# A DeepNorm encoder layer on one core: 21 of 24 projection chunks in the first stage, seven feature tiles modulated by VectorE

## The chip, the core and the metric

The kernel runs on one core of one Trainium2 chip. The metric is the device time of one execution in microseconds (us). Three timed runs of the kernel before gave 1085.3, 1085.6 and 1085.9 us, a median of 1085.61 us.

A core has a matrix engine, TensorE (PE in the profile, with its weight loads in a row of their own, PEld), a vector engine (DVE), a scalar engine (ACT), GpSimd (POOL) and a sync engine (SP). Each engine works through its own instruction list in the list's order and waits on semaphores for the others. Here almost all weights come through SP's DMA queue, in pieces of 1 MB ("chunks").

## The reference

One encoder layer for 256 tokens of width 2048: windowed attention (32 query heads, 8 key heads, width 64) and a squared-ReLU MLP, both modulated by a condition vector c.

```python
mod = silu(c) @ mod_w + mod_b                        # 2048 -> 6*2048
sh_m, sc_m, g_m, sh_f, sc_f, g_f = split(mod, 6)
h = x * (1 + sc_m) + sh_m
q, k, v = split(h @ w_qkv + b_qkv)                   # 2048 -> 3072
q, k = rope(q), rope(k)
s = where(|kpos - qpos| <= 128, q k^T / 8, -inf)
p = exp(s - m) / (sum(exp(s - m)) + exp(sink - m))
x = LN(2**.25 * x + (1 + g_m) * (p v @ w_o + b_o))
h = x * (1 + sc_f) + sh_f
x = LN(2**.25 * x + (1 + g_f) * (relu(h @ w1 + b1)**2 @ w2 + b2))
```

## The kernel before

**Arithmetic.** A float32 product is made of three fast ones (`mm3`, lines L685 to L687): weights and activations are split into a high part and a rest, and high x high, high x rest and rest x high are summed. So each weight chunk of 128x2048 needs, in two halves, a cast on ACT for the high part (`wh`, L382, in the first stage L393) and a subtraction on DVE for the rest (`wl`, L351), and then 24 matmuls of 128x512.

**First stage.** The 2048 features are 16 tiles of 128 (k = 0 to 15). For each tile, scale and shift must be computed from two chunks of `mod_w` before the tile can be used (`modulated`, L713 to L718). The two chunks are worked off in one of two ways, chosen by `MIXP`: on PE, as 16 small matmuls a chunk (L458, tile `gv`), followed by a copy and a small matmul (L556), or on DVE, as one pass over the whole chunk (L498), two passes a tile. Ten tiles go by PE and six by DVE. Meanwhile the projection to q, k, v runs. Its weight is 24 chunks, 12 of them for the first half of the columns ("units", each of four pieces of one k and 512 columns) and 12 for the other half ("quarters" (g, p): four feature tiles 4g to 4g+3, 512 columns p). `SEQ` lists the chunks that the first stage takes and the tiles whose `mod_w` chunks are loaded behind each: all 12 units and five quarters, 17 chunks. From it `first_order` makes one fixed order for PE, ACT and DVE. Eight buffers of 1 MB feed it; afterwards five are left (`RAWS`).

**Attention.** The other seven projection chunks are in `LATE`. Two of them run ahead of a loop over n = 0 to 20. Step n holds the scores of head pair group n (`scores`: PE L922, DVE L929, ACT L939), the transposes of step n-1's probabilities (`probs_T`: PE L964, ACT L966), the normalising of step n (`normalise`: DVE L947 and L951, ACT L954) and, in every second step, the product with v (`values`: PE L980, ACT L983, DVE L984). Between the pieces a step has one weight chunk of 24 matmuls: in steps 0 to 4 one of the five remaining `LATE` chunks, from step `OUT_AT` = 5 on one of the 16 chunks of the output projection (`project`). Step 5 needs the first two `values`.

**Filling.** What is left of the modulation (the attention gate: 8 row chunks for PE and 8 column chunks for DVE; then the MLP's) is planned into the stream between the weight chunks, `SLOT_FILL` giving how many for each step from n = -2 on: one each for the first seven steps, then two. A row chunk is L458 on tile `pm`, a column chunk L498 on `colm` or `modf`. In the stream row and column chunks alternate. All chunks, of whatever kind, pass through one queue on SP in the planned order, and each waits until its buffer is free.

Outside the fixed first stage, the order on each engine is made by the framework's scheduler when the kernel is built.

Of the kernel before, what the change touches and what calls it, by code (L numbers as in the profile page):

```python
# [20 lines left out]
S = 256  # L21
# [10 lines left out]
PRE = 2  # L32
OUT_AT = 5
X_AT = 11
SLOT_FILL = (1, 1, 1, 1, 1, 1, 1, 2, 2, 2, 2, 2, 2, 2, 2, 2, 2, 2, 2, 2, 1, 0, 0)
MIXG = (1,) * 16
MIXP = tuple(int(k not in (4, 6, 8, 10, 12, 14)) for k in range(16))
FFG = (4, 4, 4, 4)
FFP = (2, 2, 4, 0)
GMP = 1  # L40
# [10 lines left out]
def mod_chunks():  # L51

    out = []
    for which, sizes, prods in (("m", MIXG, MIXP), ("f", FFG, FFP)):
        k0 = 0
        for nk, p in zip(sizes, prods):
            out += [("w" + which, p, k0, i) for i in range(2 * p)]
            out += [("c" + which, n, k, 0) for k in range(k0 + p, k0 + nk) for n in range(2)]
            k0 += nk
    for which, p in (("m", GMP), ("f", 0)):  # L60
        out += [("rg" + which, h, i, 0) for h in range(p) for i in range(8)]
        out += [("cg" + which, 0, k, 0) for k in range(8 * p, NK)]
    return {c: i for i, c in enumerate(out)}


MODS = mod_chunks()
SEQ = [(0, [1, 2]), (1, [3]), (2, []), ((0, 3), [4]), ((0, 4), [5]), (3, [6]), (4, [7]), (5, []), ((1, 3), [8]), ((1, 4), [9]), (6, [10]), (7, [11]), (8, [12]), ((2, 3), [13]), (9, [14]), (10, [15]), (11, [])]
XK = {0: 2, 2: 2, 4: 4, 8: 4, 12: 4}


def first_loads():

    out = [("m", 0, 0), ("m", 0, 1)]
    for n, ks in SEQ:
        out.append(("w", n))
# [4 lines left out]
def first_order():  # L80
# [4 lines left out]
    def op(key, eng, after, rank, kind=None):  # L85
        ops[key] = eng, cost[kind or key[0]], after, rank

    for k in range(NK):
        g0, g1 = ("g", k, 0), ("g", k, 1)
        if MIXP[k]:  # L90
            op(g0, "PE", [("m", k, 0)], 0, "gP")
# [12 lines left out]
    halves, last, freed = [], {"e": [("cp", 3)]}, []  # L104
    for n, _ in SEQ:
        q = type(n) is tuple
# [20 lines left out]
    for i in range(4):  # L127
        op(("sp", i), "PE", [("cp", i - 1)] if i else [("u", SEQ[0][0], 1)], 4)
        op(("cp", i), "ACT", [("sp", i)], 0)
# [39 lines left out]
def hybrid_kernel(ctx: ExitStack, tc: tile.TileContext, a, out: bass.AP):  # L169
# [9 lines left out]
    def bank(name="pa"):  # L179
        return psum.tile([128, 512], F32, name=name, tag="bank")  # L180
# [14 lines left out]
    def g4(dt=F32):  # L195
        return gen.tile([128, 1024], dt, tag="g4", name="g4")
# [99 lines left out]
    def bias_all(src, b):  # L296

        for h in range(2):
            nc.gpsimd.dma_start(b[h], src[:, h * 1024:h * 1024 + 1024].partition_broadcast(128))
        return lambda c: b[c // 2][:, (c % 2) * 512:(c % 2) * 512 + 512]  # L300
# [134 lines left out]
    S = Stream()  # L435
# [169 lines left out]
    def groups(which, sizes, prods, mb, dst):  # L605
        out, k0 = [], 0
        for nk, p in zip(sizes, prods):
            out.append(Group(which, k0, nk, p, mb, dst))
            k0 += nk
        return out  # L610

    modm = cst.tile([128, 2, NK], F32, name="modm")
    modf = cst.tile([128, 2, NK], F32, name="modf")
    m_mix = groups("m", MIXG, MIXP, modmb, modm)
    m_ff = groups("f", FFG, FFP, modfb, modf)
    m_gm = Gate("m", GMP, gateb[:, 0])
    m_gf = Gate("f", 0, gateb[:, 1])

    LATE = [(3, 3), (2, 4), (3, 4), (0, 5), (1, 5), (2, 5), (3, 5)]
    wq = lambda g, p: S.plan(a["wqkv"][12 + (p - 3) * 4 + g])  # L620
    FIRST = first_loads()
    for v in FIRST:
# [11 lines left out]
    def plan_late(n):  # L634
        for _ in range(n):
            while lp[0] < len(late) and late[lp[0]].planned == late[lp[0]].n:
                lp[0] += 1
            if lp[0] < len(late):
                late[lp[0]].plan()

    OUTS = [(c, j) for j in range(4) for c in range(4)]
    for n in range(-PRE, OUT_AT + 16):
        plan_late(SLOT_FILL[n + PRE])
        if n == X_AT:
            S.side[len(S.q)] = lambda: load_rows()
        if n + PRE < len(LATE):
            wq(*LATE[n + PRE])
        elif n >= OUT_AT:
# [35 lines left out]
    def mm3(ps, xh, xl, wh, wl, start, stop):  # L684
        S.pinned(nc.tensor.matmul(ps, xh, wh, start=start, stop=False))  # L685
        nc.tensor.matmul(ps, xh, wl, start=False, stop=False)  # L686
        S.prev = nc.tensor.matmul(ps, xl, wh, start=False, stop=stop).ins  # L687
# [10 lines left out]
    def load_rows():  # L698

        for c in range(4):  # L700
            xs.append(g4())
            nc.sync.dma_start(xs[c].rearrange("p (t n) -> p t n", t=NT), a["x"][:, :, c * 512:c * 512 + 512])
# [80 lines left out]
        else:  # L783
            S.pinned(nc.vector.tensor_add(d, d, ps))

    BEGIN = [(3, 3), (2, 4), (0, 5)]

    def qkv(g, p):

        hh, hl = held[g]  # L790
        wh, wl = S.main()
        c = CORD[p]
        pss = half.pop(c, None) or banks()
        for k2 in (0, 2):
            for t in range(NT):
                for k in (k2, k2 + 1):
                    s = slice(k * 256 + t * 128, k * 256 + t * 128 + 128)
                    mm3(pss[t], hh[:, s], hl[:, s], wh(k), wl(k), k == 0 and (g, p) in BEGIN, False)
            S.done()
            if k2 == 0:  # L800
                yield
        if g < 3:
            half[c] = pss
        else:
            evict(c, pss)

    def run(gen, mid=()):
        next(gen)
        for f in mid:
            f()  # L810
        for _ in gen:
            pass
# [15 lines left out]
    S.loads()  # L828
    nth = {n: i for i, (n, _) in enumerate(SEQ)}
    load_of = {v: i for i, v in enumerate(FIRST)}  # L830
    for op, *v in first_order():
        if op == "g":
            k, i = v
# [19 lines left out]
        elif op == "u":  # L853
            n, i = v
# [14 lines left out]
        S.loads()  # L869
    S.passed(len(FIRST), len(SEQ))  # L870
    S.pin = S.deep = False
# [3 lines left out]
    def rope(c, which):  # L875

        A, B = acc[c], (g4b if late_tiles else g4)()
        Av = A.rearrange("p (t h d) -> p t h d", t=NT, h=8)
        Bv = B.rearrange("p (t h d) -> p t h d", t=NT, h=8)

        def tab(n):
            return trig[:, which, n, :, None, :].to_broadcast([128, NT, 8, 32])

        halves = [slice(0, 32), slice(32, 64)]
        for x in range(2):
            nc.vector.tensor_tensor(Bv[:, :, :, halves[x]], Av[:, :, :, halves[1 - x]], tab(1 + x), op=OP.mult)
        yield A
        for x in range(2):
            nc.vector.tensor_tensor(Av[:, :, :, halves[x]], Av[:, :, :, halves[x]], tab(0), op=OP.mult)
        yield A  # L890
        nc.vector.tensor_add(A, A, B)
        yield A

    def whole(gen):
        for A in gen:
            pass
        return A

    def heads_T(A):

        out = g4()
        for pr in range(2):
            pt = bank("pt")
            for i in range(2):
                for t in range(NT):
                    c = t * 512 + (pr * 2 + i) * 128
                    nc.tensor.transpose(pt[:, i * 256 + t * 128:i * 256 + t * 128 + 128], A[:, c:c + 128], ident)
            nc.scalar.copy(out[:, pr * 512:pr * 512 + 512], pt)
        return out
# [193 lines left out]
    kA = whole(rope(4, 0))  # L1103
    run(qkv(*LATE[0]))
    qA[0] = whole(rope(0, 1))
    kT = []
    run(qkv(*LATE[1]), [lambda: kT.append(heads_T(kA))])
    kT = kT[0]
# [12 lines left out]
    for n in range(OUT_AT + 16):  # L1121
        j, i = n // 4, n % 4
        if n < 16:
            scores(n)
        for f in todo:
            f()
        todo = []
        if n == 3:
            assert all(h is raws for h in S.home[S.at:]), "an early buffer is still in use"
            late_tiles.append(1)  # L1130
        w = iter(())
        if n + PRE < len(LATE):
            w = qkv(*LATE[n + PRE])
        elif n >= OUT_AT:
            if n == OUT_AT:
                bo = bias_all(a["bo"], [g4b(), g4b()])
            w = project(*OUTS[n - OUT_AT])
        mid = mids(n)
        if j < 3:
            if i == 1:  # L1140
                turn = rope(j + 1, 1)
                mid += [lambda: next(turn), lambda: next(turn)]
            if i == 2:
                mid.append(lambda: qA.__setitem__(j + 1, next(turn)))
            if i == 2:
                mid.append(lambda: qT.__setitem__(j + 1, heads_T(qA[j + 1])))
        next(w, None)
        for f in mid:
            f()
        next(w, None)  # L1150
        if 0 < n <= 16 and n % 2 == 0:
            todo.append(values(n - 1))
        if n == 11:
            g1 = m_gm.spread([g4(), g4()])
            st = [sml.tile([128, 4, 6], F32, name=f"st{t}", bufs=2) for t in range(NT)]
        if n == 17:
            ff_columns(0)
# [332 lines left out]
```

## Time and profile before

| What | Number |
|---|---|
| median of three timed runs | 1085.61 us |
| span of the profiled execution, first to last instruction | 1083.7 us |
| PE busy, DVE busy, ACT busy | 98%, 72%, 49% of the span |
| first stage ends on PE (last `mm3` of a unit) | 139.5 us |
| scores of step 0 end on PE | 166.2 us |
| first matmul of the output projection (step 5) | 210.5 us |
| end of the attention and output stage | about 345 us |
| DMA: moved in all, mean rate | 292.75 MB, 270 GB/s |

The page gives one execution on the core; a time of its own beside the span isn't listed, and the span is 1.9 us shorter than the median of the timed runs. Matmul ends are modelled, so a PE that is always busy isn't a PE at its peak; the distance between starts shows the pace.

### The profile page before, as it was taken

To read this page: it belongs to the slowest core of one execution; us is meant where nothing else is said; L and a number is where in the kernel's file an instruction comes from. 1 tells how busy PE (TensorE), PEld (TensorE's weight loads), DVE (VectorE), ACT (ScalarE), POOL (GpSimd) and SP (SyncE) were. 2 spreads that over 40 slices of the span, in tenths; PEclk is the share of its full clock that TensorE was granted. 3 is DMA by queue.
4 is the path that set the end of the run, shared out by engine and by line. 5 is a ranking of instruction groups with operands and counts; after the bars stand their busy time and mean duration, and the time that the engine had idled before them with its cause. 6 is when DMAs were issued, how large, how long until landed. Compare 5 with 4: busy or idle time off the path is not lost.

```text
span 1083.7 us, 16256 instructions
## 1 busy us (share of the span) xinstructions
PE 1064.7 (98%) x6519; PEld 881.5 (81%) x6519; DVE 785.3 (72%) x1134; ACT 527.5 (49%) x814; POOL 19.7 (2%) x41
## 2 busy tenths in 40 slices
PE   8999999999999999999999999999999999999997
PEld 6777776677777899988888888888888888888885
DVE  3587689798799888754688789656665557665795
ACT  2453348777772646633345443344553334554340
POOL 2000000000000000000000010000000000000000
PEclk9999999999999999999999999999999999999999
DMA  9999997898973997555777889756555555557522
GB/s 380 425 425 425 427 407 270 352 348 344 391 277 122 420 352 273 193 194 194 272 272 274 295 293 319 297 203 222 194 194 188 192 193 201 181 181 263 194 78 78
DMA packets 43692, 292.75 MB, mean 270 GB/s; under 512 B 4916, under 2 KB 5076, under 8 KB 9824
## 3 DMA queue, kind: packets, MB, share of 16 engines
q1 hardware_dynamic: 40256, 281.82, 69.3%
q0 software_dynamic: 2496, 8.43, 2.3%
q10 hardware_dynamic: 864, 1.45, 0.4%
q8 instruction: 51, 0.84, 0.3%
q14 instruction: 25, 0.20, 0.0%
HBM read 289.57 MB, written 2.11 MB: 269 GB/s over the span
## 4 chain that ended last, share of the span: by engine, by line
PE 91%; DVE 5%; DMA 1%; ACT 1%; issue 1%; SPq 0%; DVEq 0%; ACTq 0%
PE pa L685 17%; PE pa L687 17%; PE pa L686 16%; PE pa L1264 16%; PE pa L1266 8%; PE pa L1240 3%; PE pa L1238 3%; PE pa L1239 3%; DVE raw L498 2%; PE pm L458 2%; PE gv L458 1%; PE pa L922 1%; PE pt L964 1%; PE pa L980 1%; DMA raw<-in_mod 1%; DVE wl L351 1%
## 5 line engine op out<-in xcount | busy, mean ns | idle before, releaser
L351 DVE TENSOR_TENSOR wl<-raw,wh 128x1024 fp32r<-128x1024 f32 x332 | 403.7, 1222 | 222.4 <-ACT wh L382 205.6
L382 ACT CAST wh<-raw 128x1024 fp32r<-128x1024 f32 x298 | 311.6, 1052 | 346.3 <-PE pa L687 203.1
L685 PE MATMUL pa<-wh,g 128*128 128x512 f32 x816 | 324.1, 398 | 2.7 <-ACT g L782 1.4
L687 PE MATMUL pa<-wh,g 128*128 128x512 f32 x816 | 319.3, 391 | 0.5 <-DVE g L984 0.4
L686 PE MATMUL pa<-wl,g 128*128 128x512 f32 x816 | 319.0, 391 | 0.5 <-DVE wl L351 0.4
L1264 PE MATMUL pa<-g,wh 128*128 128x512 f32 x768 | 192.3, 392 | 0.0
L685 PEld LDWEIGHTS pa<-wh,g 128*128 128x128 f32 x816 | 153.3, 188 | 42.7 <-issue 8.2
L687 PEld LDWEIGHTS pa<-wh,g 128*128 128x128 f32 x816 | 153.3, 188 | 34.6 <-issue 1.3
L686 PEld LDWEIGHTS pa<-wl,g 128*128 128x128 f32 x816 | 153.5, 188 | 31.4 <-DVE wl L351 1.2
L1264 PEld LDWEIGHTS pa<-g,wh 128*128 128x128 f32 x768 | 138.3, 189 | 25.1 <-ACT wh L382 0.2
L498 DVE CUSTOM_DVE_ANT_0 raw<-raw,cb 128x2048 f32<-128x2048 f32 x52 | 118.5, 2283 | 9.3 <-ACT cb L868 5.6
L1266 PEld LDWEIGHTS pa<-g,wl 128*128 128x128 f32 x768 | 104.8, 190 | 7.5
L1266 PE MATMUL pa<-g,wl 128*128 128x256 f32 x768 | 107.1, 282 | 0.0
L1240 PE MATMUL pa<-g,wl 128*128 128x256 f32 x256 | 72.3, 284 | 1.9 <-DVE wl L351 1.9
L1238 PE MATMUL pa<-g,wh 128*128 128x256 f32 x256 | 72.7, 285 | 0.3 <-ACT g L1173 0.3
L1239 PE MATMUL pa<-g,wh 128*128 128x256 f32 x256 | 72.4, 284 | 0.0
L1240 PEld LDWEIGHTS pa<-g,wl 128*128 128x128 f32 x256 | 48.9, 192 | 2.1 <-DVE wl L351 2.1
L1238 PEld LDWEIGHTS pa<-g,wh 128*128 128x128 f32 x256 | 49.1, 192 | 1.0 <-ACT g L1173 0.6
L1239 PEld LDWEIGHTS pa<-g,wh 128*128 128x128 f32 x256 | 49.1, 192 | 0.4 <-issue 0.4
L393 ACT CAST wh<-raw 128x1024 fp32r<-128x1024 f32 x34 | 34.8, 1048 | 21.8 <-DMA raw<-in_wqkv 19.6
L939 ACT ACTIVATE g<-g,nm 128x256 f32<-128x256 f32 x64 | 31.8, 498 | 13.1 <-DVE nm L929 13.0
L929 DVE CUSTOM_DVE_ANT_0 g<-pa,msk,nsnk 128x256 f32<-128x256 f32 x64 | 27.1, 477 | 6.3 <-PE pa L922 6.3
(204 smaller groups left out, 743.6 us busy)
## 6 DMA issues: line engine op xcount, KB each, us to landing
raw<-in_mod SPq DMA_DIRECT2D x96, 1024.0 KB, 8.8
raw<-in_w SPq DMA_DIRECT2D x64, 1024.0 KB, 4.8
raw<-in_w1b SPq DMA_DIRECT2D x48, 1024.0 KB, 4.8
raw<-in_wqkv SPq DMA_DIRECT2D x24, 1024.0 KB, 15.3
raw<-in_wo SPq DMA_DIRECT2D x16, 1024.0 KB, 7.4
raw<-in_w1a SPq DMA_DIRECT2D x16, 1024.0 KB, 7.4
g<-in_x SPq DMA_DIRECT2D x4, 512.0 KB, 9.1
gb<-in_lnrow POOLq DMA_DIRECT2D x8, 256.0 KB, 5.7
```

Of the source, the lines that this page charges most:

```text
L351: self.pinned(nc.vector.tensor_sub(l, r, f32(self.hs[n])))
L382: self.last[n] = nc.scalar.copy(h, s)
L393: self.pinned(nc.scalar.copy(h, s))
L498: S.pinned(nc.vector.tensor_tensor_reduce(out=raw, in0=raw, in1=cb, scale=1.0, scalar=0.0, op0=OP.mult, op1=OP.add, accum_out=self.dst))
L685: S.pinned(nc.tensor.matmul(ps, xh, wh, start=start, stop=False))
L686: nc.tensor.matmul(ps, xh, wl, start=False, stop=False)
L687: S.prev = nc.tensor.matmul(ps, xl, wh, start=False, stop=stop).ins
L1238: nc.tensor.matmul(o, wh(w, 128), hh, start=new, stop=False)
L1239: nc.tensor.matmul(o, wh(w, 128), hl, start=False, stop=False)
L1240: nc.tensor.matmul(o, wl(w, 128), hh, start=False, stop=end)
L1264: nc.tensor.matmul(ps, wh(k, 128), ff_in(k), start=k == 0, stop=False)
L1266: nc.tensor.matmul(ps[:, :256], wl(k, 128), ff_in(k)[:, :256], start=False, stop=k == NK - 1)
```

## The change

The first stage takes four more projection chunks, the quarters (0,5), (1,5), (2,5) and (2,4): 21 of 24. `LATE` keeps three, (3,3), (3,4) and (3,5). Seven tiles (6, 7, 9, 11, 12, 13, 15) instead of six (4, 6, 8, 10, 12, 14) are modulated by DVE passes. The load order in `SEQ` is another one. `SLOT_FILL` moves modulation chunks ahead: 1, 1, 2, 3, 2, 2, 2, ... instead of 1, 1, 1, 1, 1, 1, 1, 2, ...; its sum stays 34. Steps 1 to 4 of the attention loop have no weight chunk any more, since `LATE` is used up by step 0 and the output projection still begins at step 5; there the loop calls the stream three times (`S.pump(1)`) around the softmax pieces.

```diff
-SLOT_FILL = (1, 1, 1, 1, 1, 1, 1, 2, 2, 2, 2, 2, 2, 2, 2, 2, 2, 2, 2, 2, 1, 0, 0)
+SLOT_FILL = (1, 1, 2, 3, 2, 2, 2, 2, 2, 2, 2, 2, 2, 1, 2, 1, 1, 1, 1, 1, 1, 0, 0)
-MIXP = tuple(int(k not in (4, 6, 8, 10, 12, 14)) for k in range(16))
+MIXP = tuple(int(k not in (6, 7, 9, 11, 12, 13, 15)) for k in range(16))
-SEQ = [(0, [1, 2]), (1, [3]), (2, []), ((0, 3), [4]), ((0, 4), [5]), (3, [6]), (4, [7]), (5, []), ((1, 3), [8]), ((1, 4), [9]), (6, [10]), (7, [11]), (8, [12]), ((2, 3), [13]), (9, [14]), (10, [15]), (11, [])]
+SEQ = [(0, []), (1, [1, 2, 3]), (2, []), ((0, 5), []), ((0, 3), []), (3, [4, 5, 6]), ((0, 4), []), (4, [7]), ((1, 4), []), (5, []), ((1, 5), [8]), (6, [9]), ((1, 3), []), (7, [10, 11]), ((2, 5), []), (8, [12]), ((2, 3), []), (9, [13]), ((2, 4), [14]), (10, []), (11, [15])]
-    LATE = [(3, 3), (2, 4), (3, 4), (0, 5), (1, 5), (2, 5), (3, 5)]
+    LATE = [(3, 3), (3, 4), (3, 5)]
-    BEGIN = [(3, 3), (2, 4), (0, 5)]
+    BEGIN = LATE
+        if n + PRE >= len(LATE) and n < OUT_AT:
+            S.pump(1)
+            for f in mid[:1]:
+                f()
+            S.pump(1)
+            for f in mid[1:]:
+                f()
+            S.pump(1)
         next(w, None)
-        for f in mid:
+        for f in mid if n + PRE < len(LATE) or n >= OUT_AT else ():
             f()
```

**PE, from the scores of step 0 to those of step 1.** Before, the projection chunk of step 0 ends, the bias matmuls (L292) close it, the scores of step 1 follow (L922), and the next projection chunk stands right behind them (L685 to L687).

```order
L687 MATMUL pa<-wh,g_1115 128x512
L292 MATMUL pa<-g_127,g_129 128x512 x2
L922 MATMUL pa<-g_1497,g_1526 128x256 x4
L685 MATMUL pa<-wh,g_255 128x512
L686 MATMUL pa<-wl,g_255 128x512
L687 MATMUL pa<-wh,g_256 128x512
```

In the changed kernel the same place reads so; `pm` is the row chunks' tile, 8 rows a chunk for the gate (so the 32 are gate row chunks 5 to 8) and 16 rows for the MLP's, and L586 the transposes of the finished gate rows.

```order
L687 MATMUL pa<-wh,g_1230 128x512
L292 MATMUL pa<-g_127,g_129 128x512 x2
L458 MATMUL pm<-raw,cact 32x256 x32
L586 MATMUL pt<-ident,mrow 128x128 x2
L458 MATMUL pm<-raw,cact 32x128 x16
L922 MATMUL pa<-g_1634,g_1676 128x256 x4
L964 MATMUL pt<-ident,g_1695 128x128 x8
L922 MATMUL pa<-g_1634,g_1676 128x256 x4
L458 MATMUL pm<-raw,cact 32x128 x16
L964 MATMUL pt<-ident,g_1826 128x128 x8
```

Five row chunks moved ahead of the scores of step 1, and no weight matmul stands between the scores and the transposes that wait for them.

**DVE, ahead of the scores of step 1.** Before, behind the passes of step 0's scores, there are two halves of a weight chunk (L351), one column chunk (L498, whose second row only reads the sum), the small softmax rows and two evictions (L784), and then L929 of step 1.

```order
L351 TENSOR_TENSOR wl_1573<-raw_1397,wh_1522 128x1024
L934 TENSOR_TENSOR es_1551<-nm_1546,pack_81 128x4
L498 ISA raw_1400,colm_114<-raw_1400,cb_110 128x2048
L498 ISA colm_114 128x1
L947 TENSOR_TENSOR rs_1578<-sm_1553,es_1551 128x4
L351 TENSOR_TENSOR wl_1599<-raw_1397,wh_1571 128x1024
L951 RECIPROCAL rs_1578<-rs_1578 128x4
L784 TENSOR_TENSOR g4_657<-g4_657,pa_1469 128x512
L784 TENSOR_TENSOR g4_657<-g4_657,pa_1470 128x512
L929 ISA g4_1613,nm_1614<-pa_1607,msk_140,nsnk_102 128x256
```

In the changed kernel these are the last rows ahead of step 1's first L929 (`raw_1605`, `raw_1632` and `raw_1711` hold gate column chunks 6 to 8; chunks 4 and 5 and a rotary pass of L886 to L891 stand further ahead, behind step 0's L929).

```order
L498 ISA raw_1605,colm_114<-raw_1605,cb_110 128x2048
L498 ISA colm_114 128x1
L498 ISA raw_1632,colm_114<-raw_1632,cb_110 128x2048
L498 ISA colm_114 128x1
L590 TENSOR_TENSOR colm_114<-pt_1748,pack_81 128x8
L351 TENSOR_TENSOR wl_1760<-raw_1670,wh_1756 128x1024
L351 TENSOR_TENSOR wl_1805<-raw_1670,wh_1758 128x1024
L498 ISA raw_1711,colm_114<-raw_1711,cb_110 128x2048
L498 ISA colm_114 128x1
L595 TENSOR_TENSOR colm_114<-colm_114,pack_81 128x8
L929 ISA g4_1826,nm_1827<-pa_1820,msk_140,nsnk_102 128x256
```

One column chunk ahead of step 1's scores became five, and both halves of the first output-projection chunk (`raw_1670`) stand there too.

**SP, the loads of that stretch.** In the changed kernel the queue holds, from gate column chunk 6 (first row here) on, row 7, column 7, row 8, the first output-projection chunk, column 8, the MLP's row chunk 1 and the second output-projection chunk. The bracket names the semaphores that a load waits for: `DMAHW` those of older loads, `PE` or `DVE` the engine that last reads what was in its buffer.

```order
L335 DMA raw<-in_mod 128x2048 [waits DMAHW4_49,PE_49]
L335 DMA raw<-in_mod 128x2048 [waits DVE_49]
L335 DMA raw<-in_mod 128x2048 [waits DMAHW6_49,DMAHW3_49,PE_49]
L335 DMA raw<-in_mod 128x2048 [waits DVE_49]
L335 DMA raw<-in_wo 128x2048 [waits DMAHW5_49,DMAHW0_49,PE_49]
L335 DMA raw<-in_mod 128x2048 [waits DVE_49]
L335 DMA raw<-in_mod 128x2048 [waits DMAHW7_49,DMAHW2_49,PE_49]
L335 DMA raw<-in_wo 128x2048 [waits DVE_49]
```

Before, a weight chunk stands between any two modulation chunks from step -2 to step 4; here eleven modulation chunks in a row follow the last projection chunk. With five buffers a load waits for the chunk five places ahead of it: the fourth row, row chunk 8, for the DVE pass over column chunk 5, and the seventh, the MLP's row chunk 1, for PE's work on row chunk 7.

## The prediction

> **What bounds the kernel now.** The page first: how much of the span PE fills, and what the chain that ended last consists of.
>
> ```profile
> span 1083.7 us, 16256 instructions
> PE 1064.7 (98%) x6519; PEld 881.5 (81%) x6519; DVE 785.3 (72%) x1134; ACT 527.5 (49%) x814; POOL 19.7 (2%) x41
> PE   8999999999999999999999999999999999999997
> DMA  9999997898973997555777889756555555557522
> PE 91%; DVE 5%; DMA 1%; ACT 1%; issue 1%; SPq 0%; DVEq 0%; ACTq 0%
> ```
>
> PE fills the span except for its first fortieth and its last, and it is 91% of the chain. Only work taken from PE, or PE idle time, can change much. So next comes the table of busy times by stage: the start, the rest of the first stage, the two projection chunks up to the first scores, the stretch from there to the output projection, and the rest of the attention.
>
> ```profile
> core 0: us, PE busy (x) PEld busy (x) DVE busy (x) ACT busy (x) POOL busy (x), PEclk, DMA share, GB/s
> 10.00:20.00 10.00, 7.97 (x110) 5.67 (x110) 3.53 (x6) 2.77 (x5) 0.00 (x0) 0.83 1.01 420
> 20.00:139.50 119.50, 115.34 (x960) 91.02 (x953) 81.88 (x109) 47.53 (x65) 0.00 (x0) 1.00 1.01 426
> 139.50:166.20 26.70, 26.30 (x159) 19.21 (x157) 21.97 (x24) 13.55 (x19) 1.14 (x2) 1.00 0.88 364
> 166.20:210.50 44.30, 44.03 (x283) 30.91 (x283) 37.06 (x83) 37.20 (x91) 0.00 (x0) 1.00 0.86 323
> 210.50:345.00 134.50, 134.03 (x964) 99.86 (x963) 120.67 (x249) 88.88 (x210) 2.64 (x5) 1.00 0.81 307
> ```
>
> In the first stage the DMA queue is full (1.01), yet PE idles only 4.2 us of 119.5: the two are balanced. From 166.2 to 210.5 PE idles 0.3 us, but DVE is busy for 37.1 of 44.3 and ACT for 37.2. PE bounds this stretch only because four weight chunks lie in it. Those are what the change takes away.
>
> The pace of PE is read from starts, in the timeline of a whole weight chunk:
>
> ```profile
> 133.97 0.47 PE L685 MATMUL pa<-wh,g 128*128 128x512 f32 x1
> ...
> 139.53 0.62 PE L292 MATMUL pa<-g,g 128*128 128x512 f32 x2
> ```
>
> Twenty-four matmuls take 5.56 us, 0.23 each, at full pace.
>
> **The change, part by part.**
>
> *The tile that leaves PE.* The groups of the first stage (20 to 139.5 us):
>
> ```profile
> L458 PE MATMUL gv<-raw,cact 128*32 128x128 f32 x520 | 17.8, 276 | 0.0
> L556 PE MATMUL gv<-both,mrow 128*128 128x2 f32 x18 | 2.5, 208 | 0.0
> ```
>
> One chunk is 32 of the first row, so 17.8 / 16.25 = 1.1 us; a tile has two, and 0.28 for L556 (2.5 / 9). One tile fewer on PE: -2.5 us. Its two DVE passes cost 2 x 2.28 = 4.6 us (below), beside matmuls.
>
> *Four weight chunks earlier.* Up to the scores of step 0, PE's list now holds 552 weight matmuls, before 473: 79 x 0.23 = +18.2 us. The other engines get eight more casts, eight more L351 and six more evictions. DVE then has 81.9 + 9.8 + 4.6 + 4.1 = 100 us of work in a stage of about 139 us, ACT less: hidden, except where a single pass stands in the way. The 4.2 us of PE idle may vanish or double; I take it as unchanged and keep -4 and +4. So the first scores end at 166.2 + 18.2 - 2.5 = **182 us**. The four chunks of DMA (2.45 us each at 426 GB/s) end well ahead of PE.
>
> *The stretch behind the first scores.* Its groups before:
>
> ```profile
> L351 DVE TENSOR_TENSOR wl<-raw,wh 128x1024 fp32r<-128x1024 f32 x11 | 13.4, 1215 | 2.8 <-ACT wh L382 2.8
> L498 DVE CUSTOM_DVE_ANT_0 raw<-raw,cb 128x2048 f32<-128x2048 f32 x5 | 11.4, 2282 | 0.0
> L929 DVE CUSTOM_DVE_ANT_0 g<-pa,msk,nsnk 128x256 f32<-128x256 f32 x20 | 8.5, 477 | 6.3 <-PE pa L922 6.3
> L891 DVE TENSOR_TENSOR g<-g,g 128x1024 f32<-128x1024 f32 x1 | 1.2, 1212 | 0.0
> L922 PE MATMUL pa<-g,g 64*128 64x256 f32 x40 | 5.7, 402 | 0.0
> L964 PE MATMUL pt<-ident,g 128*128 128x128 f32 x32 | 5.1, 279 | 0.3 <-ACT g L954 0.3
> L458 PE MATMUL pm<-raw,cact 128*32 128x256 f32 x64 | 4.3, 385 | 0.0
> L980 PE MATMUL pa<-g,g 128*64 128x256 f32 x32 | 3.9, 385 | 0.0
> L939 ACT ACTIVATE g<-g,nm 128x256 f32<-128x256 f32 x20 | 9.9, 498 | 1.5 <-DVE nm L929 1.4
> L954 ACT ACTIVATE g<-g,rs 128x256 f32<-128x256 f32 x20 | 8.6, 500 | 4.5 <-DVE rs L951 4.5
> L966 ACT COPY g<-pt 128x512 f32<-128x512 f32 x8 | 4.3, 573 | 0.4 <-PE pt L964 0.4
> ```
>
> PE: 104 weight matmuls become 24 (-80 x 0.23 = -18.4) and four row chunks become seven (+3 x 1.1): 44.0 - 18.4 + 3.3 = **29 us** of work. DVE, from step 0's scores to the second `values`: L351 10 to 5 (-6.1), column chunks 5 to 8 (+6.8), a whole further rotary pass (L891 here 1 to 2, with two more each of L886 and L889: +3.9). So DVE has about 42 us where it had 37, while PE has 15 less. Were every load there in time, the stretch would last **42 us** by DVE's list alone, with PE idle for 13.
>
> It will last longer, because the three lists wait for each other. How long a load takes:
>
> ```profile
> raw<-in_w1b SPq DMA_DIRECT2D x48, 1024.0 KB, 4.8
> ```
>
> 4.8 us where the queue is short, plus 2.45 for each chunk still ahead. Now the rows of the change shown above, from the end of the first scores as 0:
>
> - DVE does step 0's L929 (1.7, four at 0.43), rotary pieces and column chunk 4 by 6.2, waits for the last projection chunk on PE (24 matmuls and a row chunk, 7.3), evicts, finishes the rotary pass at 10.5 and column chunk 5 at 12.8.
> - Row chunk 8's load waits for that buffer: it lands at 12.8 + 4.8 = 17.6. Behind it in the queue come the first output-projection chunk, column 8 and the MLP's row 1: 17.6 + 3 x 2.45 = 25.0. PE, at row 8 since about 12.5, waits; it does the MLP's row chunk by 26.1 and the scores of step 1 by 27.3.
> - DVE does one L929, then stands at L351 of the second output-projection chunk (landed 27.5, cast 1.05, done 30.0), two L929, a column chunk whose load comes 2.45 later (33.0), the last L929 (33.4). Step 1's softmax ends: last exponential (0.5), L947 and L951 behind another L351 and rotary pieces (36.3), normalising (8.6 / 5 = 1.7), transposes on PE: 39.1.
> - `values` of step 1 (their copies stand behind step 2's exponentials on ACT, 41.6) end at 43.6, scores of step 3 at 44.7, their L929 at 46.3, exponentials 48.4, reciprocal 49.1, normalising 51.4, transposes and copies (1.0 + 1.1) 54.2, `values` 55.2.
>
> So the output projection starts **55 us** after the first scores, against 44.3.
>
> *Sum.* First scores +15.7; the stretch +10.9 by the chain, -2.3 by DVE's list alone; three row chunks are already done that PE did later, -3.3. That gives +23 and +10 us. The rest of the program is the same work. I lean on the chain, since each hop is in the order, but its waits are summed with every load at its latest, so I take **+20** on the span of 1083.7: 1103.7, and with the 1.9 us by which the median of 1085.6 lies above the span, **1105.6 us**.
>
> *A price that isn't in this sum.* What PE does after idling is in the timeline near the start:
>
> ```profile
> 14.94 1.08 PE L458 MATMUL gv<-raw,cact 128*32 128x128 f32 x32 [2.03 <-DMA raw<-in_mod]
> 16.56 0.63 PE L687 MATMUL pa<-wh,g 128*128 128x512 f32 x1
> 16.99 0.63 PE L685 MATMUL pa<-wh,g 128*128 128x512 f32 x1
> 17.41 0.63 PE L686 MATMUL pa<-wl,g 128*128 128x512 f32 x1
> ```
>
> Around a wait of 2.0 us the starts come 0.43 us apart instead of 0.23, and the granted clock of that window is 0.83. The Trainium skill (TensorE: Matmul & The Clock Gate, section "HAM oscillation — how this bites in real kernels") says that idle gaps over about 3.4 us put PE back to half its clock, again after each gap. By it, the waits of 5 us and more in the stretch would all be followed by slow matmuls, which speaks against this change; the row shows the effect after a shorter gap already. Worked out from rows: four such gaps, each followed by scores, transposes or `values` of the chain (1.1 to 2.0 us each, twice as long at half pace, about 1.5 us a gap): +6 us.
>
> **Rivals.**
>
> 1. *DVE's list alone*: the loads land in time and PE waits only for DVE. +10 us: 1096. For it: the DMA queue ran at 0.86 in this stretch, so it has room. Against: five buffers, and row 8's wait for a DVE pass. With the first stage's idle time gone as well, 1092.
> 2. *The clock falls in the waits*: +6 on the forecast, 1112.
> 3. *The stretch is filled* (faster): if PE doesn't wait for DVE or loads, it needs 29 us instead of 44, and the four chunks are moved at no cost: the span falls by the tile, 2.5 us, and up to 4.2 of the first stage's idle time: 1079 to 1083. It decides if the scores' chain fits into 29 us of PE work. Against it: DVE's 42 us in one list.
> 4. *Between*: only the latency of the softmax shows, with column chunks done in its gaps; a stretch of about 33 us leaves +1 or so: 1086.
>
> **Chances.** Forecast 0.52, rival 1 0.22, rival 2 0.16, rival 3 0.06, rival 4 0.04. The range must reach rivals 1 and 2: from 1091 (rival 1 with the idle time gone) to 1114 (rival 2 and the first stage a little worse). A measurement of this kernel tells some 0.2% (2.2 us) from no change. Faster by more: 0.06; within: 0.04; slower: 0.90.
>
> **What would show it.** In the changed profile: the first scores (L922) end near 182 us, and the first stage's PE idle time stays near 4 us. From there to the first L685 on the output projection it takes about 55 us, with PE idle for 26, and waits of PE on `raw<-in_mod` (L458) ahead of the second scores and on ACT's L954 ahead of L964. L929 of step 1 starts some 25 us after step 0's. The clock column under 1.00 in that stretch would speak for rival 2, PE waiting only on ACT or DVE for rival 1. I'm wrong if PE stays busy there, or if the first stage (139.5 us before, plus 96 x 0.23, minus 2.5) ends far from 159 us.

## The result, and the profile after

| | before | changed |
|---|---|---|
| median | 1085.76 us (4 runs, 1085.3 to 1086.6) | 1110.55 us (4 runs, 1109.2 to 1113.8) |
| ratio, 95% interval | | 1.0231 [1.0215, 1.0248] |
| span of the profiled execution | 1083.7 us | 1107.4 us |
| scores of step 0 end on PE | 166.2 us | 178.2 us |
| stretch from there to the first output-projection matmul | 44.3 us | 59.8 us |
| from there to the end | 873.2 us | 869.4 us |

The kernel is slower by 24.8 us. The span splits at the two marks of the prediction: +12.0 for the first scores, +15.5 for the stretch, -3.8 for the rest, +23.7 in all.

The page of the changed kernel: span, busy times, the 40 slices, the chain's shares.

```profile
span 1107.4 us, 16149 instructions
PE 1068.6 (96%) x6453; PEld 883.6 (80%) x6453; DVE 796.7 (72%) x1146; ACT 528.2 (48%) x813; POOL 19.8 (2%) x41
PE   8999998499999999999999999999999999999997
PEclk9999999689999999999999999999999999999999
PE 89%; DVE 6%; DMA 2%; ACT 1%; issue 1%; SPq 0%; DVEq 0%; ACTq 0%
```

One slice, the eighth (194 to 221 us), has a 4 where there was a 9, and the granted clock has a 6 in the same place. Apart from the slices next to it, little else differs in these two rows. The table of stages says the same in microseconds; its columns are those of the table of before.

```profile
20.00:155.80 135.80, 133.56 (x1014) 107.76 (x1013) 100.44 (x128) 57.12 (x75) 0.00 (x0) 1.00 1.01 426
155.80:178.20 22.40, 21.47 (x139) 15.51 (x137) 18.58 (x22) 9.94 (x15) 1.15 (x2) 1.00 0.74 276
178.20:238.00 59.80, 38.36 (x286) 22.33 (x284) 45.09 (x98) 30.27 (x83) 0.00 (x0) 0.74 0.85 341
238.00:371.20 133.20, 132.88 (x893) 99.89 (x892) 109.42 (x231) 88.43 (x211) 2.65 (x5) 1.00 0.67 245
```

The first stage is well filled: PE idles 2.2 us of 135.8. In the third row it idles 21.4 us of 59.8, and DVE is busy for only 45.1. The means hide what each part is short of, so here is the same stretch in four parts:

```profile
178.20:190.50 12.30, 9.23 (x76) 6.01 (x74) 12.27 (x23) 4.50 (x14) 0.00 (x0) 1.00 1.01 402
190.50:206.40 15.90, 6.39 (x66) 2.98 (x66) 9.71 (x12) 2.36 (x3) 0.00 (x0) 0.50 1.00 409
206.40:225.00 18.60, 12.26 (x92) 8.04 (x88) 15.14 (x34) 11.88 (x31) 0.00 (x0) 0.69 0.93 374
225.00:238.00 13.00, 10.49 (x58) 5.29 (x56) 7.97 (x30) 11.52 (x35) 0.00 (x0) 0.87 0.40 153
```

The DMA queue is full (1.01 and 1.00) up to the scores of step 1, while PE waits for row chunks, and nearly full (0.93) in the next part; its mean of 0.85 comes from the last 13 us (0.40). The waits of PE in this stretch, by what it waited for (total, times, longest):

```profile
PE pm L458 <- DMA raw<-in_mod: 13.6, 4, 4.6
PE pt L964 <- ACT g L954: 6.6, 3, 3.6
PE pt L907 <- DVE es L934: 0.6, 1, 0.6
PE pt L586 <- ACT mrow L584: 0.5, 1, 0.5
```

And in order of time, each with what it waited for in brackets:

```profile
185.49 1.93 PE L458 MATMUL pm<-raw,cact 128*32 128x256 f32 x32
190.58 1.94 PE L458 MATMUL pm<-raw,cact 128*32 128x256 f32 x16 [3.16 <-DMA raw<-in_mod]
197.11 1.93 PE L458 MATMUL pm<-raw,cact 128*32 128x256 f32 x16 [4.59 <-DMA raw<-in_mod]
...
204.56 1.93 PE L458 MATMUL pm<-raw,cact 128*32 128x128 f32 x32 [4.34 <-DMA raw<-in_mod]
206.43 1.73 PE L922 MATMUL pa<-g,g 64*128 64x256 f32 x8
208.09 1.10 PE L964 MATMUL pt<-ident,g 128*128 128x128 f32 x8
```

Step 1's scores stand at 206.43. The transposes of step 0's probabilities (L964) come at 208.09, 30 us after step 0's scores, and wait for nothing there: they had only been standing behind row chunks that waited for their loads.

### The profile page after: what moved, and what is told of

It reads as the page before. It is cut to its first block, busy times and chain, and to the rows that moved or that the text cites. A ratio compares the mean times of both kernels' runs of the same rounds, so it can differ in the third digit from the quotient of the medians.

```text
span 1107.4 us, 16149 instructions
## 1 busy us (share of the span) xinstructions
PE 1068.6 (96%) x6453; PEld 883.6 (80%) x6453; DVE 796.7 (72%) x1146; ACT 528.2 (48%) x813; POOL 19.8 (2%) x41
## 4 chain that ended last, share of the span: by engine, by line
PE 89%; DVE 6%; DMA 2%; ACT 1%; issue 1%; SPq 0%; DVEq 0%; ACTq 0%
PE pa L685 17%; PE pa L687 17%; PE pa L686 16%; PE pa L1272 16%; PE pa L1274 8%; PE pa L1248 3%; PE pa L1246 3%; PE pa L1247 3%; DMA raw<-in_mod 2%; PE gv L458 1%; DVE raw L498 1%; PE pa L980 1%; PE pm L458 1%; PE pa L922 1%; PE pt L964 1%
## 5 line engine op out<-in xcount | busy, mean ns | idle before, releaser
L351 DVE TENSOR_TENSOR wl<-raw,wh 128x1024 fp32r<-128x1024 f32 x332 | 403.2, 1223 | 216.2 <-ACT wh L382 202.0
L685 PE MATMUL pa<-wh,g 128*128 128x512 f32 x816 | 322.5, 396 | 1.7 <-ACT g L713 0.9
L687 PE MATMUL pa<-wh,g 128*128 128x512 f32 x816 | 318.3, 390 | 0.3 <-DVE g L984 0.3
L685 PEld LDWEIGHTS pa<-wh,g 128*128 128x128 f32 x816 | 153.2, 188 | 40.3 <-issue 6.2
L687 PEld LDWEIGHTS pa<-wh,g 128*128 128x128 f32 x816 | 153.2, 188 | 33.3 <-DVE g L984 1.0
L498 DVE CUSTOM_DVE_ANT_0 raw<-raw,cb 128x2048 f32<-128x2048 f32 x54 | 123.3, 2286 | 7.6 <-DMA raw<-in_mod 7.4
L458 PE MATMUL pm<-raw,cact 128*32 128x256 f32 (+1 forms) x512 | 27.5, 354 | 13.6 <-DMA raw<-in_mod 13.6
```

What stands on the lines that cost most here:

```text
L351: self.pinned(nc.vector.tensor_sub(l, r, f32(self.hs[n])))
L458: i = nc.tensor.matmul(self.ps[32 * j:32 * j + 32, :w], lhsT[j] if type(lhsT) is list else lhsT, rhs[j], start=self.first, stop=stop)
L498: S.pinned(nc.vector.tensor_tensor_reduce(out=raw, in0=raw, in1=cb, scale=1.0, scalar=0.0, op0=OP.mult, op1=OP.add, accum_out=self.dst))
```

## The experiments

**Order alone.** The stream may not pass the start of slot n's chunks before step n. The work and the planned order of the loads stay as they are; the row chunks then stand behind step 1's scores.

```diff
     for n in range(-PRE, OUT_AT + 16):
+        begins[n] = len(S.q)
         plan_late(SLOT_FILL[n + PRE])
...
-    S.stop = len(S.q)
+    S.stop, ends = begins[1], len(S.q)
...
             scores(n)
+        if n > 0:
+            S.stop = begins[n + 1] if n < OUT_AT - 1 else ends
```

> The changed kernel's work, with one thing different: the stream may not pass the start of slot n's chunks before step n, so the scores of step 1 stand right behind step 0's projection chunk in PE's list and the row chunks behind them. Theory A (the row chunks ahead of the scores, and their loads, hold the chain of scores and softmax): step 1's scores end about 9 us after step 0's instead of 30, the stretch from the first scores to the output projection falls from 59.8 us to about 45, where DVE's list of 45.1 us bounds it, and the time to 1095 to 1098 us. Rival B (the four chunks that are gone were the only filling, PE has nothing else to do): the stretch stays between 55 and 60 us and the time between 1106 and 1111 us.

1091.54 us, ratio to before 1.0054 [1.0037, 1.0071]: 19 us of the 24.8 are gone. The held kernel's stretch in the table of stages, and its timeline on PE:

```profile
178.20:216.10 37.90, 31.40 (x241) 18.30 (x238) 33.48 (x92) 28.89 (x90) 0.00 (x0) 0.95 0.85 333
```

```profile
185.86 1.13 PE L924 MATMUL pa<-g,g 64*128 64x256 f32 x8
186.93 1.07 PE L458 MATMUL pm<-raw,cact 128*32 128x256 f32 x16
187.93 0.87 PE L966 MATMUL pt<-ident,g 128*128 128x128 f32 x6
```

(L924 and L966 are L922 and L964, two lines further down.) Step 1's scores come 20.6 us sooner and the transposes behind them 20.2 us sooner. The stretch is 37.9 us (37.1 from the end of its own first scores, at 179.0), shorter than theory A gave, and the time lies 3.5 us below theory A's range: DVE's 45.1 us were no bound, since part of its work moved behind the stretch (33.5 stayed). Two row chunks of the MLP moved there too: from the output projection to the end it takes 874.0 us, 4.6 more than in the changed kernel. Rival B falls, for no weight matmul was added.

**Fewer chunks in the stretch.**

```diff
-SLOT_FILL = (1, 1, 2, 3, 2, 2, 2, 2, 2, 2, 2, 2, 2, 1, 2, 1, 1, 1, 1, 1, 1, 0, 0)
+SLOT_FILL = (1, 1, 0, 0, 0, 0, 0, 3, 3, 3, 3, 3, 2, 2, 2, 2, 2, 2, 2, 2, 1, 0, 0)
```

> The changed kernel with SLOT_FILL at 0 for steps 0 to 4 (these chunks go to steps 5 to 9, behind the stretch): only the modulation chunks that are fetched ahead remain between the first scores and the output projection. Theory A: what is left is the softmax's own latency, a stretch of 33 to 38 us, that is 22 to 27 us less than 59.8; PE later has about five row chunks more (5.5 us); the time falls to 1089 to 1095 us, still above the kernel before. Rival B (missing weight chunks alone): PE idles as long as now, the stretch falls only by the moved row chunks, 5.5 us, which come back later, so about 1110 us. Rival C (DVE's list): the stretch falls by the four column passes of 2.28 us that leave it, 9 us, and the time to about 1101 to 1106 us.

1099.36 us, 1.0124 [1.0109, 1.0139]. None of the three had it: faster than B and C said, slower than A. The stretch:

```profile
178.00:221.10 43.10, 33.53 (x188) 19.62 (x186) 34.61 (x85) 28.22 (x82) 0.00 (x0) 0.80 0.70 256
```

The waits for loads are gone, but 43.1 us are no bare latency. PE waits 8.6 us for ACT's normalising (L954), and DVE's timeline of step 0's softmax shows what it waits behind: between the maximum's row (L934) and the sum's (L947) stand a column chunk of 2.29 us and a rotary piece.

```profile
183.47 0.15 DVE L934 TENSOR_TENSOR es<-nm,pack 128x4 f32<-128x4 f32 x1
183.55 1.29 DVE L889 TENSOR_TENSOR g<-g,trig 128x512 f32<-128x512 f32 x2
184.75 2.29 DVE L498 CUSTOM_DVE_ANT_0 raw<-raw,cb 128x2048 f32<-128x2048 f32 x1
186.96 0.09 DVE L498 DVE_READ_ACCUMULATOR2_ANT colm<- 128x1 f32 x1
186.96 0.16 DVE L947 TENSOR_TENSOR rs<-sm,es 128x4 f32<-128x4 f32 x1
```

So the order on DVE prices the chain too. The moved row chunks came back later: from the output projection to the end it took 876.1 us, 6.7 more than in the changed kernel (5.5 expected).

**Less work for DVE.**

```diff
-GMP = 1
+GMP = 2
...
-            nc.vector.tensor_tensor(d, d, b, op=OP.add)
+            if self.p < 2:
+                nc.vector.tensor_tensor(d, d, b, op=OP.add)
```

> The changed kernel with the whole attention gate as row chunks on PE (GMP = 2): eight DVE passes of 2.28 us (18 us in all) leave DVE, eight row chunks of 1.1 us (8.8 us) come to PE. Theory A (order and loads hold the chain): the scores of step 1 still stand behind row chunks that wait for their loads, so the stretch loses 0 to 6 us of its 59.8, and the row chunks ahead of it add up to 4 us: 1106 to 1113 us. Rival C (DVE's list sets the stretch): five passes fewer in it, 11 us less, about 1100 us.

1104.69 us, 1.0173 [1.0155, 1.0192]: between the two, nearer to theory A by the time, but not by its parts. The stretch falls by 14.7 to 45.1 us, more than rival C's 11; but the first scores end at 189.0 us instead of 178.2, because 12 row chunks come ahead of them (192 records, 16 a chunk, in the group up to 189 us) instead of three. The stage and the group:

```profile
189.00:234.10 45.10, 35.98 (x271) 20.96 (x269) 30.65 (x83) 28.46 (x79) 0.00 (x0) 0.81 0.81 327
```

```profile
L458 PE MATMUL pm<-raw,cact 128*32 128x256 f32 x192 | 12.0, 383 | 2.0 <-DMA raw<-in_mod 2.0
```

PE's waits for loads in it are 4.0 us instead of 13.6. That DVE's passes had held the buffers isn't shown by this, since fewer gate chunks were left in the stretch as well. The experiment doesn't separate the two.

**The clock.** Matmuls on the identity, in columns of tile `pm` that nobody reads, fill the waits ahead of the row chunks; the numbers are how many, by row chunk, counted from 0 (6 is gate row chunk 7).

```diff
+WARM = {6: 28, 7: 48, 8: 48, 9: 10}
+WARM_END = {9: 32}
...
             last = self.i == self.n
+            self.lead = self.idle(WARM.get(len(rowsdone), 0), i == 0) if not self.at else None
...
+                d = nc.tensor.matmul(self.ps[:, 256:384], ident, ident, start=new, stop=new).ins
```

> The changed kernel with matmuls on the identity (tile pm, columns that nobody reads) put ahead of the waiting row chunks: 28 ahead of gate row chunk 7, 48 ahead of row chunk 8, 48 ahead of the MLP's row 1, 10 ahead of its row 2 and 32 behind it, at about 0.1 us each a little less than the waits they stand in; no other work is changed. Theory (the clock that falls in the waits is part of the loss): row chunks take 1.07 us again instead of 1.93, step 1's scores 1.13 instead of 1.73, its values about 2 instead of 3.4; what stands ahead of a load that is late anyway is hidden, the rest is 4 us, so 1105 to 1108 us, and the granted clock of the stretch above 0.9 instead of 0.74. Rival (the waits alone set the length of the stretch): 1109.5 to 1112 us with the clock back.

1124.96 us, 1.0374 [1.0356, 1.0391]: a miss of the experiment. One such matmul took 0.23 us, not the 0.1 that I had read off the transposes, so the filling outlasted the loads. The second one has 13, 21 and 22 of them, ahead of gate rows 7 and 8 and the MLP's row 1.

```diff
-WARM = {6: 28, 7: 48, 8: 48, 9: 10}
-WARM_END = {9: 32}
+WARM = {6: 13, 7: 21, 8: 22}
+WARM_END = {}
```

> As warm, with matmuls on the identity that fit into the waits: in warm one of them took 0.23 us, not 0.1, so they outlasted the loads by some 10 us. Now 13 ahead of gate row chunk 7 (3.0 us), 21 ahead of row chunk 8 (4.9 us) and 22 ahead of the MLP's row 1 (5.1 us), and none ahead of or behind its row 2. DVE's order behind step 1's scores shifts a little with them (its four L929 stand together, ahead of the second output-projection chunk's casts). Theory (the clock that falls in the waits is part of the loss): row 1, step 1's scores and its transposes at full pace, step 1's scores end 1 to 2 us earlier, its values 3 to 5 us: 1105 to 1108 us. Rival (the waits alone set the length of the stretch): 1109.5 to 1112 us. Below 1104 us it would be the shifted L929 that gained, not the clock.

1109.38 us, 1.0208 [1.0187, 1.0229], beside 1.0231 [1.0215, 1.0248] for the changed kernel: the intervals overlap, so no gain can be told. The median is just below the rival's range, and one execution of the four (1105.7) lies in the theory's. Its timeline (L500 is the filling, L462, L943, L985, L1001 are L458, L922, L964, L980):

```profile
192.92 4.96 PE L500 MATMUL pm<-ident 128*128 128x128 f32 x42
197.81 1.07 PE L462 MATMUL pm<-raw,cact 128*32 128x256 f32 x16
...
199.64 5.08 PE L500 MATMUL pm<-ident 128*128 128x128 f32 x44
204.65 1.13 PE L943 MATMUL pa<-g,g 64*128 64x256 f32 x8
...
218.84 1.95 PE L1001 MATMUL pa<-g,g 128*64 128x256 f32 x16
...
228.16 0.69 PE L985 MATMUL pt<-ident,g 128*128 128x128 f32 x2 [4.22 <-ACT g L975]
```

The slow matmuls are fast again: row chunk 8 takes 1.07 us instead of 1.93, step 1's scores 1.13 instead of 1.73, its `values` 1.95 instead of 3.39, and these start 2.9 us sooner (218.84, in the changed kernel 221.77). PE then waits 4.2 us for ACT where it had waited 2.4, and still starts the transposes behind that wait 3.2 us sooner (228.16, in the changed kernel 231.37). Yet the output projection starts at 237.4 instead of 238.0, only 0.6 sooner. Its stretch among the stages, and the time from those transposes to the output projection, first in this kernel and then in the changed one:

```profile
178.20:237.40 59.20, 48.10 (x395) 33.23 (x393) 43.16 (x100) 29.93 (x83) 0.00 (x0) 0.88 0.82 323
228.00:237.40 9.40, 9.24 (x32) 4.12 (x32) 2.55 (x14) 5.54 (x17) 0.00 (x0) 0.51 0.24 99
231.30:238.00 6.70, 6.63 (x32) 3.06 (x32) 3.34 (x9) 5.43 (x17) 0.00 (x0) 0.75 0.43 157
```

The same 32 matmul records take 9.4 us at a clock of 0.51 and 6.7 at 0.75. So the clock was not given back to the end: it fell again behind the wait of 4.2 us, and there the gain was lost. Where the filling held the clock, the chain gained some 3 us; what a full clock up to the output projection would be worth, this experiment doesn't tell. DVE's order shifted a little with the filling, and the first scores end half a microsecond sooner here (at 177.7), so neither 0.6 nor 3 us is a pure measure.

**The change's parts.** Next, the changed kernel with `SLOT_FILL` as before, and the kernel before with the new `SLOT_FILL`. The first:

```diff
-SLOT_FILL = (1, 1, 2, 3, 2, 2, 2, 2, 2, 2, 2, 2, 2, 1, 2, 1, 1, 1, 1, 1, 1, 0, 0)
+SLOT_FILL = (1, 1, 1, 1, 1, 1, 1, 2, 2, 2, 2, 2, 2, 2, 2, 2, 2, 2, 2, 2, 1, 0, 0)
```

> The changed kernel with the SLOT_FILL of the kernel before, the other parts of the change as they are: 21 chunks in the first stage and seven tiles by DVE. Step 1's scores then stand behind one row chunk instead of five, and five modulation chunks are planned into steps 0 to 4 instead of eleven. Theory A (what stands ahead of the scores costs the time, not the missing weight chunks): the stretch is 40 to 45 us instead of 59.8, some six row chunks come back later (6 us), so 1095 to 1101 us. Rival B (the steps lack filling, and SLOT_FILL's early chunks were a help): the stretch stays at 55 us or more, 1108 to 1116 us.

1093.79 us, 1.0082 [1.0067, 1.0097], a little below both of theory A's ranges; the stretch is 39.0 us and what follows takes 873.9, 4.5 us more than in the changed kernel:

```profile
178.70:217.70 39.00, 30.97 (x195) 18.13 (x195) 33.87 (x83) 28.04 (x78) 0.00 (x0) 0.87 0.82 306
```

Theory A holds against rival B. The second experiment is the same edit the other way round, in the kernel before:

```diff
-SLOT_FILL = (1, 1, 1, 1, 1, 1, 1, 2, 2, 2, 2, 2, 2, 2, 2, 2, 2, 2, 2, 2, 1, 0, 0)
+SLOT_FILL = (1, 1, 2, 3, 2, 2, 2, 2, 2, 2, 2, 2, 2, 1, 2, 1, 1, 1, 1, 1, 1, 0, 0)
```

> The kernel before with the changed kernel's SLOT_FILL alone. Up to step 1, PE's list has the same order as before; three row chunks more come ahead of step 2's scores, among weight matmuls. Theory A (the early chunks only cost where no weight matmuls stand between them and the scores): within 4 us of the kernel before, 1084 to 1090 us. Rival (eleven modulation chunks and their loads in these steps are too many for five buffers in any case): the stretch grows by 8 us or more, later work falls by 3, so 1091 us or more.

1097.34 us, 1.0106 [1.0091, 1.0121]: theory A is wrong here, +12.0 us although all weight chunks are still there. The rival had the time and the longer stretch, but not the reason: no wait of PE in the stretch is for a load. The stretch in the stages, and DVE's timeline of its costly pieces:

```profile
164.60:221.80 57.20, 51.83 (x334) 34.22 (x332) 43.02 (x89) 36.12 (x89) 0.00 (x0) 0.94 0.86 322
```

```profile
183.70 0.45 DVE L929 CUSTOM_DVE_ANT_0 g<-pa,msk,nsnk 128x256 f32<-128x256 f32 x1
...
188.62 2.36 DVE L351 TENSOR_TENSOR wl<-raw,wh 128x1024 fp32r<-128x1024 f32 x2 [0.56 <-ACT wh L382]
190.89 2.28 DVE L498 CUSTOM_DVE_ANT_0 raw<-raw,cb 128x2048 f32<-128x2048 f32 x1
193.10 2.35 DVE L351 TENSOR_TENSOR wl<-raw,wh 128x1024 fp32r<-128x1024 f32 x2
195.38 2.28 DVE L498 CUSTOM_DVE_ANT_0 raw<-raw,cb 128x2048 f32<-128x2048 f32 x1
...
211.07 0.48 DVE L929 CUSTOM_DVE_ANT_0 g<-pa,msk,nsnk 128x256 f32<-128x256 f32 x1
```

From step 2's softmax (its first rows at 183.7, its small rows up to 188) to step 3's (211.1) DVE works off hardly anything but weight halves and column chunks, and stands idle for some 10 us of it; before, step 3's scores began 24.5 us after the end of step 0's (190.67 - 166.2), here 43.2 (207.77 - 164.6). PE has weight matmuls meanwhile, and they and three row chunks stand ahead of the chain in its list: the transposes of step 1's probabilities, which ACT had normalised by 185.6, come at 204.05 and wait for nothing there (before, they came at 181.84). When the chain goes on, the weight matmuls are used up: PE's longest wait is 3.2 us, behind step 3's L929. So other work gets ahead of the chain here as well, and the filling is used up too early. Of the 12.9 us by which the stretch is longer, 5.1 are PE's idle time. The rest is a longer busy time: two more row chunks (2.1 us), seven more records of weight matmuls, since the first scores end 1.6 us sooner (1.6 us), and a clock of 0.94, by estimate 3.4 us (0.06 of 57.2); some matmuls of `values` moved out of it.

**The cast ahead of the output projection.** In `hold` PE stands 3.3 us for the first cast of that weight.

```diff
-            S.stop = begins[n + 1] if n < OUT_AT - 1 else ends
+            S.stop = begins[n + 1] if n < OUT_AT - 2 else ends
```

> The kernel held back by slots (hold), with the stream freed one step sooner, so that the first output-projection chunk may be cast during step 3. In hold PE stood 3.5 us at its first output-projection matmul, for that cast on ACT (L382). If that wait is a loss of its own: 1087.5 to 1089 us. If ACT or DVE then do that cast in place of softmax rows that are waited for: 1090.5 to 1093 us.

1094.09 us, 1.0078 [1.0063, 1.0093]: 2.5 us more than `hold` by the medians, with intervals that overlap. The wait at the cast is gone and a new one stands behind the stretch, again a row chunk ahead of the transposes, waiting for its load:

```profile
246.60 1.93 PE L458 MATMUL pm<-raw,cact 128*32 128x128 f32 x32 [4.00 <-DMA raw<-in_mod]
```

**The seventh tile, and an eighth.** In the kernel before, alone:

```diff
-MIXP = tuple(int(k not in (4, 6, 8, 10, 12, 14)) for k in range(16))
+MIXP = tuple(int(k not in (4, 6, 8, 10, 12, 13, 14)) for k in range(16))
```

> The kernel before with tile 13 modulated by two DVE passes as well (seven tiles, everything else as before). The step of the prediction: PE loses 2.5 us of the first stage and DVE's 4.6 us lie beside matmuls, so 1083 us. Rival: the first stage is bound by the loads (DMA share 1.01) and the tile's two passes delay PE as much as they save: 1085.5 to 1088 us.

1084.09 us (10 runs), 0.9983 [0.9973, 0.9992]: 1.7 us faster than the kernel before, between the step's 1083 and the rival's range. With tile 15 added to the list:

> The kernel before with tiles 13 and 15 by DVE passes as well, eight in all. By the seventh tile's measure (1.7 us): 1082 to 1083.5 us. Rival (the loads bind the first stage, or the last tile's passes are waited for at its end, since tile 15 comes last): 1084.5 us or more.

1084.22 us, 0.9981 [0.9971, 0.9991]: nothing more is gained. PE's waits from 20 to 139 us show why; this row isn't among those of before:

```profile
PE pa L686 <- DVE wl L351: 4.4, 2, 2.5
```

With seven tiles the same row has 0.8 us. The passes now delay weight halves behind them on DVE: PE idles 7.7 us of the first stage from 20 us on, where with seven tiles it idles 5.2. The difference is the 2.5 us that the tile was to save PE.

**How many chunks.** The changed kernel with `SLOT_FILL` as before, and fewer quarters in the first stage; for 19:

```diff
-SEQ = [..., (7, [10, 11]), ((2, 5), []), (8, [12]), ((2, 3), []), (9, [13]), ((2, 4), [14]), (10, []), (11, [15])]
+SEQ = [..., (7, [10, 11]), (8, [12]), ((2, 3), []), (9, [13]), (10, [14]), (11, [15])]
-    LATE = [(3, 3), (3, 4), (3, 5)]
+    LATE = [(3, 3), (2, 4), (3, 4), (2, 5), (3, 5)]
-    BEGIN = LATE
+    BEGIN = [(3, 3), (2, 4), (2, 5)]
```

> The changed kernel with 19 chunks in the first stage instead of 21 (the quarters (2,5) and (2,4) late again) and SLOT_FILL as before; seven tiles by DVE. Two of the five steps then have no weight chunk, not four. Theory A (the softmax chain takes 37 to 40 us whatever lies in it; chunks may leave the stretch at no cost as long as PE's work in it is that long, here 29 - 2 + 11 us): 1082.5 to 1086 us. Rival (each moved chunk loses its share of old_fill's 8 us over the kernel before): 1088 to 1090 us.

1094.40 us, 1.0067 [1.0042, 1.0092], outside both ranges. Its four runs differ much, 1089.4 and 1094.2 to 1095.4, and the profiled one is the fastest. In it the stretch takes some 41 us, with one long wait:

```profile
207.33 1.12 PE L964 MATMUL pt<-ident,g 128*128 128x128 f32 x4 [5.62 <-ACT g L954]
```

For 18, quarter (1,5) becomes late too.

> The changed kernel with 18 chunks in the first stage (quarters (1,5), (2,5) and (2,4) late again) and SLOT_FILL as before; seven tiles by DVE. One of the steps 0 to 4 has no weight chunk. Theory A (the stretch has a floor of 37 to 40 us, given by the softmax chain): with 24 matmuls fewer than before, PE's work in the stretch is about 44 - 5.5 = 38.5 us, so at the floor, and the chunk is moved at no cost beside the seventh tile's gain: 1083 to 1086 us. Rival (each chunk that leaves the stretch costs about 2 us, wherever it stands): 1086.5 to 1089 us.

1087.27 us (12 runs from 1085.3 to 1090.2), 1.0012 [1.0003, 1.0021]: in the rival's range. The profiled run (1085.7) has a stretch of 38.5 us with PE busy for 36.1, as theory A has it:

```profile
169.70:208.20 38.50, 36.13 (x242) 24.46 (x240) 35.71 (x82) 30.59 (x79) 0.00 (x0) 1.00 0.88 331
```

With seven tiles, 17, 18, 19 and 21 chunks under the old fill give 1084.1, 1087.3, 1094.4 and 1093.8 us (17 with the load order and the tiles of `seventh_tile`). No number of moved chunks brought anything. The runs of 18 and 19 scatter by 5 to 6 us, and the granted clock on record goes with it: for 18 chunks it is 0.999 at 1085.3 us and 0.994 at 1090.2, for 19 it is 0.996 at 1089.4 and 0.990 or 0.991 in the other three. So PE worked at the lower clock for longer in the longer executions; what came first, a longer wait or the clock, can't be read from one profile each. It stays open, and with it whether the floor of the stretch or a price for each chunk sets these two.

## Why the prediction was right, and where its sizes were off

**The sign and the place were right.** The stretch behind the first scores decides, PE waits there for row chunks' loads ahead of step 1's scores and then for L954 ahead of L964, as the hops had it. `hold` shows it: with the same work in another order, 19 of the 24.8 us go. What is left without it is a stretch of 37.9 us, or 39.0 in `old_fill`. PE idles 21.4 us of the stretch where 26 were predicted, and is busy for 38.4 where 29 were: part of what was forecast as waiting was work at a lower clock.

**First scores, +15.7 predicted, +12.0 measured.** The first stage ends at 155.8 us, where 159 was predicted. PE's idle time from 20 us to the first scores fell from 4.6 to 3.2 us, where I had taken it as unchanged. Another 1.7 us, by estimate, are a term that the prediction left out: its own row from 10 to 20 us has a clock of 0.83, and in the changed kernel that row has 1.00, so matmuls that were slow there are not. The tile alone was worth 1.7 us in `seventh_tile` (2.5 predicted). Between 0.6 and 1.4 us stay unexplained, by whether the tile is taken at 2.5 or at 1.7.

**The stretch, +10.9 by the chain, +15.5 measured.** The hops came in order, each a little late. From the end of the first scores, in us:

| Hop | predicted | measured |
|---|---|---|
| row chunk 8 landed | 17.6 | 18.9 |
| the MLP's row 1 landed | 25.0 | 26.2 |
| scores of step 1 end | 27.3 | 29.9 |
| transposes of step 1 (L964) end | 39.1 | 41.1 |
| `values` of step 1 end | 43.6 | 47.0 |
| first output-projection matmul | 55 | 59.8 |

Row chunk 8's load was issued at 190.8 us, 12.6 from the mark, as its buffer came free (12.8 predicted), and the MLP's row 1 starts 7.45 us behind row 8, three places in the queue at 2.45 each. Since the queue was full in all that time, a buffer that came free sooner need not have brought the row chunks sooner; no run separates the two. The loads landed 1.3 and 1.2 us later than I had them; with the slow matmuls behind them the chain is 3.4 us late by `values`, and the last 1.4 us come in steps 2 and 3, whose transposes and `values` PE did piece by piece as ACT released them. (In the last hop the prediction's own figures slip by 0.7 us: 51.4 + 1.0 + 1.1 is 53.5, not 54.2.) I had taken 20 us where the terms summed to 23, because every load stood there at its latest. That was the wrong way round, since the loads came later still. The sum of 23.3 was nearly the measured 23.7, but by luck: an error of 3.7 us in the first scores and one of 4.6 in the stretch cancel in it.

**The clock, rival 2.** It fell as the rows near the start foretold, to 0.74 over the stretch, and PE's chain matmuls took 1.5 to 1.8 times as long. The time, 1110.6, lies near the 1112 of that rival, and nearer to it than to the forecast. Its price of 6 us isn't shown: `warm_short` gave the clock back to the matmuls up to step 1's `values` and moved these by 2.9 us; behind them the clock fell again, and the output projection moved by 0.6. A sum that hits the time isn't evidence for its terms.

**The other rivals.** DVE's list alone (rival 1) did not set the stretch: DVE is busy for 45.1 us of 59.8, and once the order is mended its chunks move out of the stretch (33.5 of 37.9 us in `hold`). That rival's premise, that the queue has room, fails too: the queue was full (1.01 and 1.00) up to step 1's scores. The filled stretch (rival 3) does not come about with 21 chunks in either order: PE idles 6.5 us in `hold` and 8.0 in `old_fill`. The latency alone (rival 4) was put at 33 us of stretch; with the order mended it comes to 38 or 39.

**The rest, -3.3 predicted, -3.8 measured**, the three row chunks.

**What the prediction hadn't split** is the change itself. By the medians of their own comparison the new `SLOT_FILL` costs 12.0 us by itself, the rest of the change 8.5 by itself, and both 24.8: together some 4 us more than the sum. My account put the loss on weight chunks that were missing around the scores; `new_fill` shows that the early modulation chunks cost about half of it with every weight chunk in place.

## What to carry to other kernels

Work that fills an engine's gaps should stand behind the instruction that starts the next wait, not ahead of it: an in-order engine turns a late load of the filling into a delay of the chain it was to cover. When weight chunks are moved out of a stretch that hides a latency chain, ask first how long that chain is by itself (about 38 us here, with 44 of work before): what is taken beyond the difference should be paid again at the new place. That last is argued, not shown: with 18 chunks the stretch was at that length, and the time was still 3.2 us above that with 17. And test the parts of such a change apart, in both kernels; the part that only looked like an adjustment was the dearer one (12.0 us against 8.5).

## What the runs showed of the hardware

A float32 matmul of 128x128 on the identity took 0.23 us from start to start (42 in 4.96 us count as 21 instructions, two records each), where the transposes of the same shape take 0.14 (eight in 1.10 us). After a wait of 3.2 us a row chunk took 1.94 us instead of 1.07. In `new_fill` a wait of 1.7 us was enough: behind it weight matmuls start 0.43 us apart (190.49, 190.91, 191.34) instead of 0.23. Matmuls put into the waits held the granted clock at full pace there (step 1's scores 1.13 us instead of 1.73), but not behind the next wait of 4.2 us (0.51): the stretch had 0.88 instead of 0.74, and the output projection began 0.6 us sooner.
